# Decode step taken apart, full-depth Strassen in the heads and first convolutions, and two buffers resized by one slot and four tiles

## The chip, the cores and the metric

The kernel runs on one core of one Trainium2 chip. The metric is the device time of one execution in microseconds (us), lower is better. The kernel before was timed three times: 2169.92, 2166.01 and 2169.59 us, median 2169.59 us. One further execution was recorded by the hardware profiler; all durations of single instructions below are from that one.

## The reference, cut to what matters

Two layers of a decoder trunk run over 512 prompt positions and 8 sample streams of one new token each, with shared weights. All data is float32.

```python
h = rmsnorm(x, norm_g)
z = h @ w_in                       # 2048 x 8192: [B, C, xc, g_conv | q, k, v, g_ret]
conv = short_conv(c_c * x_c)       # width 3, causal
y_conv = b_c * conv * silu(g_c)
q, k = rope(q), rope(k) / 16       # 4 heads of 256
# one token per sample stream, S is the state (256 x 256) of a head:
inter = (q @ S) * gamma            # what the old state gives
intra = (q . k) * v                # what the new token gives itself
S_new = gamma * S + k^T v          # an output, for each layer, stream, head
y_ret = groupnorm(inter + intra) * gn_g * silu(g_r)
x = x + concat(y_conv, y_ret) @ w_out
x = x + sigmoid(x @ w_pg) * (p @ w_ple)
```

The prompt's retention goes in chunks; its arithmetic is not touched here. The sample streams have 2 layers x 4 heads x 8 streams = 64 states of 256 x 256 float32 (256 KB each); every one has to be read, updated and written out once.

## The kernel before, in words

**Layout.** Activations lie transposed: a tile ("slot") is 128 rows of the model dimension by 520 columns, 512 prompt positions and 8 samples. There are 75 slots, handed out first-in first-out (`Slots`, L80). The model dimension of 2048 is 16 tiles deep, here called 16 K tiles.

**A product in three.** Each float32 operand is split into a rounded high part and a remainder, by ScalarE (L229 for weights, L551 for activations) and VectorE (L230, L552). A product is then three TensorE matmuls, high x high, high x low and low x high (`mm3`, L247 to L249), each 128 x 128 by 260 columns, half a slot. Raw weights come in by DMA from the SyncE queue (L222, L312) into a ring of 32 tiles; the split weights go into a second ring of 60 tiles (`SPLIT`), each chunk of up to 4 tiles taking one range for the high and one for the low part.

**A pair of output tiles.** `pair` (L396) makes two output tiles of 128 rows by 520. With `rows[n]` = 0 it calls `plain` (L270): 16 K tiles x 2 outputs x 2 halves = 64 products. With `rows[n]` = s it calls `strassen` (L290): the first s K tiles go as 2 x 2 blocks with seven block products of s/2 products each, and the remaining 16 - s K tiles go plainly with four products each, so 7s/2 + 4(16 - s) products. Strassen needs sums of weight tiles, four passes over s/2 tiles on VectorE (L319), and sums of activation tiles, four tiles for each two K tiles, made once by `operand_sums` (L410) and kept in slots. For s < 16 it uses a fourth PSUM bank c, and two products' results are combined after the plain rest (L385 to L389); for s = 16 three banks do.

**Stages of a layer.** The lists HEADS, CONVS, OUT_ROWS and GATES (L53 to L59) hold s for each pair of each layer, in order.
- *Heads*: 4 heads x 4 pairs (q, k, v, gate), `head` (L801), `retain` (L817). The pairs that carry s = 14 are 12 in the first layer and 15 in the second.
- *Convolutions*: 8 x 2 pairs (L1077). The first two and the last have s = 14, the 13 between have s = 16.
- *OUT*: 8 pairs of the output projection (L1130).
- *GATE*: 8 pairs of the gated embedding in the first layer (L1175), 7 in the second, whose last two tiles go another way in the tail (from L1215).

Between pairs, and at fixed points inside them, short jobs are run from two lists: everything in `middle` near the middle of a pair (L365), and one job of `later` at two points of each pair (`aside`, L265). The prompt's retention is cut into nine steps per head that go through `later`. Activations of the next stage are made ahead by `fill` (L468) when slots are free, and by `need` (L483) when a pair can't do without them.

**The decode step before.** For each (head, stream): `sample_load` (L768) takes two slots and loads the state and, repeated on all 128 partitions, the rows for q and k from a DRAM tile kq. One call later `sample_step` (L774) scales the state by gamma on ScalarE (L776), adds k times v in two VectorE instructions (L780), sends the new state to o_rets (L781), and takes q times the new state, summed, in two more (L784, into `osum`). Everything of it lies in the heads and convolutions, from 50.5 us (the first state load) to 1731.3 us. In the last convolution `sample_norm` (L1364) normalises all of `osum`.

**What sets the order.** Instructions are not issued as written: a planner orders each engine's list by priority (order of writing, with weight splits and sums put ahead) and by the times at which it expects operands to be ready. Each engine then runs its list strictly in that order, and waits where an operand is late. All DMAs of activations and states go through the GpSimd queue (`SIDE`), in its own order.

## Time and profile before

| | |
|---|---|
| three runs, us | 2169.92, 2166.01, 2169.59 (median 2169.59) |
| profiled execution: span, first to last instruction, us | 2167.3 |
| TensorE matmuls | 17861, busy 2147.8 us (99%) |
| VectorE busy | 1896.1 us (87%) |
| ScalarE busy | 1264.5 us (58%) |
| GpSimd busy, with its DMA issues | 430.6 us (20%) |
| DMA | 387.31 MB, mean 179 GB/s |
| granted TensorE clock, mean | 0.999 |

The profile gives no other time of its own execution than the span; it lies between the lowest and the highest of the three runs. "Busy" is the union of an engine's instructions. A matmul of 260 columns is shown with some 0.28 us, but its successor starts 0.12 us after it: they are pipelined, so that the number of matmuls that start in a stretch says more than the busy share. A line of a group reads: source line, engine, operation, output <- inputs, shape and count, then busy time and mean duration of one, then the idle time of the engine ahead of these instructions and what ended it. A line of the windows gives, for a stretch, busy us and count of each engine, the granted clock, the DMA engines' busy share and their GB/s.

In this execution the first layer's heads run to about 400 us, its convolutions to about 715, OUT to about 890, GATE to about 1100; the second layer's to about 1460, 1790, 1960 and 2100, and the tail to the end.

### The profile page before, as it was taken

Reading aid. Unit: us, or ns where it says so; the run is one execution under the profiler, and the core shown is the slowest. Engines: PE = TensorE matmul, PEld = TensorE weight load, DVE = VectorE, ACT = ScalarE, POOL = GpSimd, SP = SyncE. Lnnn points to the kernel's source line nnn. Section 1 sums busy time; section 2 is a strip of 40 time slices with the busy share of each in tenths; the row PEclk is TensorE's granted clock in tenths of the full one; section 3 lists DMA queues with packets and bytes.
Section 4 is the critical chain, followed back from the end, with each engine's and each line's share of the span. In section 5 each row is a group of like instructions: output and inputs, shape, how many; then the busy total and the mean of one; then the engine's idle time right before and its main releaser. Section 6 shows DMA issues by size and latency. Waiting matters only on the chain. (4 is left out here: it accounts for less than half of the span.)

```text
span 2167.3 us, 48178 instructions
## 1 busy us (share of the span) xinstructions
PE 2147.8 (99%) x17861; PEld 2142.1 (99%) x17861; DVE 1896.1 (87%) x3849; ACT 1264.5 (58%) x2647; POOL 430.6 (20%) x746
## 2 busy tenths in 40 slices
PE   9999999999999999999999999999999999999998
PEld 9999999999999999999999999999999999999998
DVE  8889988998999987987997988989999998879884
ACT  8656655565555655655765655565645555456565
POOL 2313222211001211200212222231111022011011
PEclk9999999999999999999999999999999999999999
DMA  8555565545543745645645566664464355566455
GB/s 288 171 175 197 181 217 184 178 157 175 158 129 118 238 156 187 215 154 160 215 144 175 172 213 191 189 209 170 151 182 149 120 158 202 176 207 200 128 164 198
DMA packets 182861, 387.31 MB, mean 179 GB/s; under 512 B 25888, under 2 KB 56352, under 8 KB 182624
## 3 DMA queue, kind: packets, MB, share of 16 engines
q1 hardware_dynamic: 128704, 212.98, 31.6%
q0 software_dynamic: 53056, 169.84, 23.8%
q8 instruction: 140, 2.29, 0.4%
q10 hardware_dynamic: 864, 1.39, 0.2%
q14 instruction: 97, 0.79, 0.1%
HBM read 318.96 MB, written 65.15 MB: 177 GB/s over the span
## 5 line engine op out<-in xcount | busy, mean ns | idle before, releaser
L247 PE MATMUL ps_g<-slot,split 128*128 128x260 f32 x5465 | 1531.6, 284 | 7.2 <-ACT slot L307 2.9
L248 PE MATMUL ps_g<-slot,split 128*128 128x260 f32 x5465 | 1534.3, 282 | 0.3 <-DVE slot L555 0.3
L249 PE MATMUL ps_g<-slot,split 128*128 128x260 f32 x5461 | 1519.9, 283 | 0.5 <-DVE split L230 0.5
L229 ACT ACTIVATE split<-raw 128x512 fp32r<-128x512 f32 (+2 forms) x1347 | 777.3, 596 | 583.1 <-DVE raw L319 213.2
L247 PEld LDWEIGHTS ps_g<-slot,split 128*128 128x128 f32 x5465 | 1024.0, 188 | 10.1 <-ACT slot L307 3.7
L248 PEld LDWEIGHTS ps_g<-slot,split 128*128 128x128 f32 x5465 | 1028.5, 188 | 0.5 <-DVE slot L555 0.5
L249 PEld LDWEIGHTS ps_g<-slot,split 128*128 128x128 f32 x5461 | 1019.8, 188 | 1.0 <-DVE split L230 1.0
L230 DVE TENSOR_TENSOR split<-raw,split 128x512 fp32r<-128x512 f32 (+2 forms) x1346 | 849.2, 652 | 172.5 <-PE ps_g L248 85.4
L319 DVE TENSOR_TENSOR raw<-raw 128x512 f32<-128x512 f32 (+1 forms) x660 | 428.9, 660 | 32.5 <-DMA raw<-wi 23.7
L307 ACT ACTIVATE slot<-ps_g 128x260 f32<-128x260 f32 x336 | 127.4, 381 | 140.6 <-PE ps_g L249 122.7
L551 ACT ACTIVATE slot<-slot 128x520 fp32r<-128x520 f32 (+1 forms) x212 | 109.2, 562 | 46.6 <-DVE slot L414 11.1
L552 DVE TENSOR_TENSOR slot<-slot,slot 128x520 fp32r<-128x520 f32 (+1 forms) x212 | 124.4, 620 | 4.1 <-ACT slot L551 3.9
L781 POOL DMA_DIRECT2D o_rets<-slot x64 | 35.3, 552 | 351.6 <-DVE slot L780 131.7
L307 DVE TENSOR_TENSOR slot<-ps_g,slot 128x260 f32<-128x260 f32 x168 | 70.9, 424 | 6.0 <-PE ps_g L249 3.7
L869 POOL DMA_DIRECT2D slot<-hs x64 | 46.2, 724 | 118.7 <-DVE split L230 42.7
L814 POOL DMA_DIRECT2D hs<-slot x64 | 35.6, 556 | 139.3 <-DVE slot L755 61.3
L780 DVE SCALAR_TENSOR_TENSOR slot<-slot,vs,slot 128x256 f32<-128x256 f32 x128 | 56.1, 481 | 4.5 <-ACT slot L776 4.3
L746 DVE TENSOR_TENSOR slot<-slot,slot 128x520 f32<-128x520 f32 x80 | 55.8, 698 | 4.7 <-DMA o_rets<-slot 3.7
L770 POOL DMA_DIRECT2D slot<-sret x64 | 35.5, 554 | 114.6 <-ACT split L229 37.3
L1058 POOL DMA_DIRECT2D slot<-x1s x76 | 40.8, 538 | 87.6 <-PE ps_g L249 27.2
L1209 POOL DMA_DIRECT2D x2s<-slot x30 | 16.4, 545 | 201.6 <-DVE slot L1204 200.6
L771 POOL DMA_DIRECT2D slot<-kq x64 | 34.9, 547 | 106.0 <-DVE slot L876 22.2
(217 smaller groups left out, 1733.8 us busy)
## 6 DMA issues: line engine op xcount, KB each, us to landing
raw<-wi SPq DMA_DIRECT2D x377, 256.0 KB, 3.9
raw<-wo SPq DMA_DIRECT2D x128, 256.0 KB, 5.4
raw<-wg SPq DMA_DIRECT2D x122, 256.0 KB, 4.1
raw<-wi SPq DMA_DIRECT2D x136, 192.0 KB, 4.0
slot<-x1s POOLq DMA_DIRECT2D x76, 260.0 KB, 5.1
slot<-sret POOLq DMA_DIRECT2D x64, 256.0 KB, 4.0
hs<-slot POOLq DMA_DIRECT2D x64, 256.0 KB, 4.0
slot<-hs POOLq DMA_DIRECT2D x64, 256.0 KB, 5.2
```

Source lines behind the costliest of these rows:

```text
L229: S.activation(hi, raw, AF.Copy)
L230: V.tensor_tensor(lo, raw, F(hi), SUB)
L247: PE.matmul(out, wh, xh, start=start, stop=False, skip_group_check=more)
L248: PE.matmul(out, wh, xl, start=False, stop=False, skip_group_check=more)
L249: PE.matmul(out, wl, xh, start=False, stop=stop, skip_group_check=more)
L307: fn(*args)
L319: V.tensor_tensor(out[:, n], x[:, n], y[:, n], op)
L551: keep(S.activation(hi, src[:, n], AF.Copy))
L552: V.tensor_tensor(lo, src[:, n], F(hi), SUB)
L746: V.tensor_tensor(out[:, n], v, table[:, n], MUL)
L780: keep(V.scalar_tensor_tensor(st[:, c], k, vs[:, h, e, b : b + 1], st[:, c], MUL, ADD))
L869: SIDE.dma_start(t[:, :512].rearrange("p (m n) -> p m n", m=2), src)
```

## The change

- **Rows of Strassen.** In the heads s becomes 16 where it was 14 (12 + 15 pairs), and in the convolutions of each layer the first two pairs go from 14 to 16 (2 x 2 pairs); the last stays 14. These are 31 pairs.
- **The decode step is taken apart.** In the heads and convolutions only gamma times q times the *old* state is taken (`sample_step`, two reducing VectorE instructions with gamma as a constant). The new token's own part, (q . k) v, is made for all streams at once in `sample_norm`: q times k elementwise into a new small tile `qk` (one VectorE instruction per head), summed over partitions by two float32 matmuls with ones of 32 columns each, times `vs`, added to `osum`.
- **The new states are made in OUT and GATE**, by `update`, a pipeline of three: `key_load` takes a slot and loads the k row, repeated on all partitions, into its right half; at the next call `state_add` makes k times v in two ScalarE instructions and issues a DMA that *adds* the old state from DRAM onto the slot; at the next call `state_out` scales by gamma on ScalarE and sends the slot to o_rets. `vs` now carries v / 16 / gamma, so that gamma (S + k v / gamma) is the new state. `update` is called in the middle and at the end of each pair of OUT and GATE and, in four of the eight OUT pairs, once more through `later`: 20 calls in OUT, 16 in the first layer's GATE and 14 in the second's, for 32 states and two calls of pipeline.
- **Loads.** One slot of queries now serves two streams.
- **Sizes.** 76 slots for 75, 56 split tiles for 60; the constant tile `vec` loses its gamma columns.

```diff
-NSLOT = 75
+NSLOT = 76
...
+GAMMA = [1.0 - 2.0 ** (-5 - h) for h in range(H)]
-HEADS = [[0, 0, 0, 8] + [14] * 12, [0] + [14] * 15]
-CONVS = [[14] * 2 + [16] * 13 + [14]] * 2
+HEADS = [[0, 0, 0, 8] + [16] * 12, [0] + [16] * 15]
+CONVS = [[16] * 15 + [14]] * 2
...
-SPLIT = 60
+SPLIT = 56
...
         def sample_load(h, b):
-            st, kb = get(), get()
+            st = get()
             SIDE.dma_start(st[:, :512], sret[l, h, b])
-            SIDE.dma_start(kb[:, :512], kq[l, h, b].rearrange("c d -> (c d)").partition_broadcast(P))
-            return h, b, st, kb
-
-        def sample_step(h, b, st, kb):
-            keep(S.activation(st[:, :512], st[:, :512], AF.Identity, scale=gam(h)))
-            k = kb[:, 256:512]
+            if b % 2 == 0:
+                queries.append(get())
+                src = kq[l, h, b : b + 2, :2].rearrange("b c d -> b (c d)").partition_broadcast(P)
+                SIDE.dma_start(queries[-1][:, :512].rearrange("p (b c) -> p b c", b=2), src)
+            return h, b, st, queries[-1]
+
+        def sample_step(h, b, st, q):
             for e in range(2):
                 c = slice(256 * e, 256 * e + 256)
-                keep(V.scalar_tensor_tensor(st[:, c], k, vs[:, h, e, b : b + 1], st[:, c], MUL, ADD))
-            SIDE.dma_start(o_rets[l, h, b], st[:, :512])
-            for e in range(2):
-                c = slice(256 * e, 256 * e + 256)
-                V.tensor_tensor_reduce(k, st[:, c], kb[:, :256], 1.0, 0.0, MUL, ADD, osum[:, e, h, b : b + 1])
-            put(st, kb)
+                n = slice(256 * (b % 2), 256 * (b % 2) + 256)
+                keep(V.tensor_tensor_reduce(st[:, c], st[:, c], q[:, n], GAMMA[h], 0.0, MUL, ADD, osum[:, e, h, b : b + 1]))
+            put(st)
+            if b % 2:
+                put(q)
...
+        def key_load(h, b):
+            st = get()
+            SIDE.dma_start(st[:, 256:512], kq[l, h, b, 2:].rearrange("c d -> (c d)").partition_broadcast(P))
+            return h, b, st
+
+        def state_add(h, b, st):
+            for e in range(2):
+                c = slice(256 * e, 256 * e + 256)
+                keep(S.activation(st[:, c], st[:, 256:512], AF.Copy, scale=vs[:, h, e, b : b + 1]))
+            SIDE.dma_start(st[:, :512], sret[l, h, b], accum_op=ADD)
+            return h, b, st
+
+        def state_out(h, b, st):
+            keep(S.activation(st[:, :512], st[:, :512], AF.Copy, scale=GAMMA[h]))
+            SIDE.dma_start(o_rets[l, h, b], st[:, :512])
+            put(st)
+
+        keyed, added = [], []
+
+        def update():
+            if added:
+                state_out(*added.pop(0))
+            if keyed:
+                added.append(state_add(*keyed.pop(0)))
+            if states:
+                keyed.append(key_load(*states.pop(0)))
+
+        states = [(h, b) for h in range(H) for b in range(NS)]
...
+            V.scalar_tensor_tensor(qk[:, :, h], qks[:, :2, :NS], GAMMA[h], qks[:, 2:, :NS], MUL, MUL)
...
-                V.scalar_tensor_tensor(vs[:, h, e, :], t[:, SEQ:T], 1.0 / 16, rb[:, SEQ:T], MUL, MUL)
+                V.scalar_tensor_tensor(vs[:, h, e, :], t[:, SEQ:T], 1.0 / 16 / GAMMA[h], rb[:, SEQ:T], MUL, MUL)
...
             middle.append(lambda: O.fill(MORE_OUT, 0))
+            middle.append(update)
+            if m % 4:
+                later.append(update)
             zs = pair(O, wo[l], m, m // 2, Gt)
+            update()
...
             middle.append(lambda: Gt.fill(MORE_GATE, 0))
+            middle.append(update)
...
             Gt.fill(MORE_GATE, 0)
+            update()
             Gt.need(m // 2 + 1)
...
-def sample_norm(nc, small, pr, osum, onesd, half_neg, gs, gn):
+def sample_norm(nc, small, pr, osum, qk, vs, ones, onesd, half_neg, gs, gn):
...
+    ps = pr.tile([P, 512], F32, tag="r", name="ps_qk")
+    for d in range(2):
+        PE.matmul(ps[:, :n], ones, qk[:, d].rearrange("p h b -> p (h b)"), start=d == 0, stop=d == 1)
+    own = small.tile([P, 2, H, NS], F32, tag="sq", name="own", bufs=1)
+    for e in range(2):
+        V.tensor_tensor(own[:, e], vs[:, :, e], ps[:, :n].rearrange("p (h b) -> p h b", b=NS), MUL)
+        V.tensor_tensor(osum[:, e], osum[:, e], own[:, e], ADD)
```

More of the change, by code (lines that the diff above doesn't have):

```diff
@@ L558, in split @@
         return op
-    vec = const.tile([P, 160], F32, name="vec")
+    vec = const.tile([P, P], F32, name="vec")
     def norm_g(l, k):
@@ L578, in kd @@
         return vec[:, c : c + 1]
-    def gam(h):
-        return vec[:, 128 + h : 129 + h]
     ident = const.tile([P, P], F32, name="ident")
@@ L590, in trunk_kernel @@
     osum = const.tile([P, 2, H, NS], F32, name="osum")
+    qk = const.tile([P, 2, H, NS], F32, name="qk")
     gs = const.tile([P, 2 * H, NS], F32, name="gs")
@@ L679, in trunk_kernel @@
             DMA.dma_start(raw.rearrange("p (m n) -> p m n", n=P), wi[0, 0:4, :, :P].rearrange("m p n -> p m n"))
-            S.dma_start(vec, vecs)
+            S.dma_start(vec, vecs[:, :P])
             x = get()
@@ L1104, in trunk_kernel @@
                 O.ready = 7
-                sample_norm(nc, small, pr, osum, onesd, half_neg, gs, lambda k: gn_g(l, k))
+                sample_norm(nc, small, pr, osum, qk, vs, ones, onesd, half_neg, gs, lambda k: gn_g(l, k))
             zg, zb = pair(X, wi[l], mt + 2, mt // 2 + 1 - skipped, O)
@@ L1359, in trunk_kernel @@
             block_out(1)
+        assert not (todo or loaded or states or keyed or added)
         if l < DEPTH - 1:
             X.ready = KT // 2
-def sample_norm(nc, small, pr, osum, onesd, half_neg, gs, gn):
+def sample_norm(nc, small, pr, osum, qk, vs, ones, onesd, half_neg, gs, gn):
     V, G, PE = nc.vector, nc.gpsimd, nc.tensor
```

2 lines of the change are left out of this document (1 added, 1 removed).

## The prediction

> **What bounds the kernel now.** I read the page's head first, then the groups of instructions by shape, then busy time by stage, and the waits and the chain last.
>
> ```profile
> span 2167.3 us, 48178 instructions
> ...
> PE 2147.8 (99%) x17861; PEld 2142.1 (99%) x17861; DVE 1896.1 (87%) x3849; ACT 1264.5 (58%) x2647; POOL 430.6 (20%) x746
> ```
>
> TensorE is busy 99%, which alone says little, since its matmuls overlap. The stretches below say how many start (the x behind PE); their columns are PE, PEld, DVE, ACT and POOL busy, clock, DMA share, GB/s.
>
> ```profile
> 200.00:250.00 50.00, 50.00 (x420) 50.00 (x419) 47.05 (x101) 30.28 (x67) 10.12 (x17) 1.00 0.60 184
> 60.00:400.00 340.00, 340.00 (x2837) 339.45 (x2837) 306.31 (x673) 201.48 (x443) 94.42 (x163) 1.00 0.59 188
> 400.00:700.00 300.00, 299.06 (x2498) 298.88 (x2497) 273.85 (x550) 164.63 (x334) 42.34 (x63) 1.00 0.49 150
> 700.00:730.00 30.00, 26.68 (x218) 26.07 (x218) 30.00 (x65) 24.88 (x68) 10.58 (x20) 1.00 0.81 272
> 730.00:890.00 160.00, 160.00 (x1337) 159.98 (x1336) 133.95 (x242) 84.92 (x169) 28.52 (x54) 1.00 0.59 192
> 890.00:1100.00 210.00, 210.00 (x1756) 210.00 (x1755) 183.43 (x361) 134.23 (x257) 33.83 (x63) 1.00 0.56 178
> 1100.00:1460.00 360.00, 359.39 (x2999) 358.41 (x2998) 317.89 (x697) 210.53 (x470) 93.21 (x156) 1.00 0.59 182
> 1460.00:1730.00 270.00, 269.12 (x2241) 268.08 (x2241) 246.83 (x493) 147.66 (x304) 37.01 (x63) 1.00 0.50 158
> 1775.00:1800.00 25.00, 23.15 (x191) 22.72 (x191) 24.66 (x55) 18.24 (x51) 7.99 (x15) 1.00 0.87 305
> ```
>
> In an undisturbed stretch 420 matmuls start in 50 us: one in 0.1190 us, 8.4 in a us. At that pace the two stretches of heads (second and seventh row) lack 2856 - 2837 = 19 and 3024 - 2999 = 25 matmuls, 5.2 us; the convolutions (third and eighth) 22 and 27, 5.8 us; the two passages into OUT (fourth and last) 34 and 19, 6.3 us; the OUT and GATE rows only 7 and 8. So TensorE's work sets the end: a matmul taken away is worth 0.119 us, and VectorE or ScalarE work taken away is worth something only out of those few lost microseconds.
>
> ```profile
> L247 PE MATMUL ps_g<-slot,split 128*128 128x260 f32 x5437 | 1523.6, 284 | 7.2 <-ACT slot L307 2.9 <-ACT ps_g L307 1.6 <-ACT split L229 1.5
> L230 DVE TENSOR_TENSOR split<-raw,split 128x512 fp32r<-128x512 f32 x1031 | 695.0, 690 | 147.8 <-PE ps_g L248 81.2 <-ACT split L229 51.8 <-issue 6.1
> L319 DVE TENSOR_TENSOR raw<-raw 128x512 f32<-128x512 f32 x520 | 354.1, 688 | 17.6 <-DMA raw<-wi 12.1 <-DMA raw<-wo 2.9
> L230 DVE TENSOR_TENSOR split<-raw,split 128x384 fp32r<-128x384 f32 x249 | 137.1, 555 | 16.2 <-ACT split L229 9.9 <-PE ps_g L248 3.4 <-ACT slot L551 1.9
> L319 DVE TENSOR_TENSOR raw<-raw 128x384 f32<-128x384 f32 x140 | 77.4, 554 | 14.9 <-DMA raw<-wi 11.6 <-DMA raw<-wg 2.8
> L230 DVE TENSOR_TENSOR split<-raw,split 128x256 fp32r<-128x256 f32 x66 | 27.3, 423 | 8.5 <-ACT split L229 7.6 <-PE ps_g L248 0.8
> L780 DVE SCALAR_TENSOR_TENSOR slot<-slot,vs,slot 128x256 f32<-128x256 f32 x128 | 56.1, 481 | 4.5 <-ACT slot L776 4.3
> L784 DVE CUSTOM_DVE_ANT_0 slot<-slot,slot 128x256 f32<-128x256 f32 x128 | 53.9, 421 | 0.0
> L776 ACT ACTIVATE slot<-slot,vec 128x512 f32<-128x512 f32 x64 | 45.7, 714 | 0.0
> L874 ACT ACTIVATE slot<-slot 128x512 fp32r<-128x512 f32 x48 | 28.7, 624 | 10.1 <-DMA yc<-slot 4.6 <-DVE slot L904 2.4 <-DVE osum L784 2.1
> L917 ACT ACTIVATE slot<-ps_kt,vec 128x256 fp32r<-128x256 f32 x32 | 15.0, 468 | 9.2 <-DMA hs<-slot 3.2 <-DVE slot L918 2.5 <-PE ps_kt L913 2.2
> ```
>
> The first row bears the count that the change acts on. A pair has 7s/2 + 4(16 - s) products (64 for s = 0): 57 at s = 14, 56 at s = 16. Summed over the lists of rows, with the 30 fourth products of the embedding that also go to these banks, that is 5437, the row's count. The weight splits on VectorE wait 81.2 us for TensorE (second row): the ring of split weights is usually full, VectorE is ahead.
>
> **The change, part by part.**
>
> *Strassen rows.* 31 pairs lose one product each, three matmuls: 93 x 0.119 = **11.1 us less**. This is the firm term. The Trainium skill (TensorE: Matmul & The Clock Gate, Back-to-back issue gap) gives N/2.4 + 2.5 ns for a warm isolated gap, by our estimate 110.8 ns at 260 columns and 10.3 us for the 93; the trace has 119.0 ns, and I keep that.
>
> VectorE pays for it. A pair's four sums and seven splits go over 8 tiles (4 + 4) in place of 7 (3 + 4), less the two plain chunks of 256 columns: 4 x (688 - 554) + 7 x (690 - 555) - 2 x 423 = 635 ns a pair, 20 us over 31 pairs. It lies beside matmuls, in stages where VectorE is busy 88 to 91%; without cover it would be 0.6 us a pair. ScalarE saves one bank copy a pair. Three PSUM banks in place of four leave one more free at each pair's end; I count nothing for it.
>
> *Sums made earlier.* The eighth pair of K tiles needs its sums before the second Strassen pair of the heads, where they could be made later. Two loads, two scalings, four half-tile sums and two splits, once a layer: nothing if `fill` has made them by then, some 3 us a layer in the worst case, as much as all that these heads now lose. I take 0.
>
> *The decode step leaves the heads and convolutions.* 128 instructions of L780 (56.1 us of VectorE) and 64 of L776 (45.7 us of ScalarE) go; the 128 of L784 stay, with a constant and another place to write. Some 16 small instructions of under 0.25 us come in. With the 20 us above, VectorE is relieved by about 33 us over the two layers, 11 in a layer's convolutions (some 13 of its 32 steps fall there). That can give back what waits there for VectorE: between 0 and the 5.8 us. The chain through the worst stretch shows both kinds of wait,
>
> ```profile
> 1693.65 0.68 DVE split L230
> 1694.33 0.61 DVE raw L319
> 1695.01 3.75 DMA raw<-wi
> ...
> 1706.59 0.88 DVE slot L780 x2
> ...
> 1717.32 3.63 DMA raw<-wi
> ```
>
> VectorE's queue and late raw weights, and only the first is helped: I take a third, **1.9 us less**.
>
> *sample_norm* gains two matmuls of 32 columns a layer, just like the pair that is there:
>
> ```profile
> 1734.53 0.53 PE L1371 MATMUL ps_sm<-osum,onesd 128*128 128x32 f32 x4
> 1734.89 0.37 PE L247 MATMUL ps_g<-slot,split 128*128 128x260 f32 x1
> ```
>
> Two calls are four instructions, 0.36 us to the next matmul's start, and that one's successor comes 0.08 us later than usual: 0.45 us a layer, **0.9 us more**. The rest of the chain there ends some 25 us before its result is read in OUT.
>
> *The new states in OUT and GATE.* For each state: two ScalarE instructions of 256 columns (nearest row L917, 468 ns) and one of 512 (L874, 624 ns), 1.56 us, 50 us a layer. ScalarE is busy 84.92 of 160 us in OUT and 134.23 of 210 in the first GATE; with 20 and 16 calls it would be 72 to 76%, still beside matmuls. On the GpSimd queue come three issues a state where one and a half (64 + 32 for 64 states) stay behind, each near 0.55 us: 192 issues, 106 us over the stages of OUT and GATE, where it is busy under a fifth. The queue is in order: the adding DMA waits for `state_add`, the store for `state_out`, and behind them stand the loads of the stage's activations, for which the splits at L551 wait, and TensorE at the next pair. ScalarE is in order too: `state_add` waits for its key row and `state_out` for the sum to land, and behind them stand weight splits. What covers both is the ring: 56 tiles are seven chunks high and low, 7 x 12 matmuls x 0.119 = 10.0 us ahead. With 60 tiles and chunks of four it was seven as well, so I cost the smaller ring at nothing.
>
> ```profile
> slot<-sret POOLq DMA_DIRECT2D x64, 256.0 KB, 4.0
> raw<-wo SPq DMA_DIRECT2D x128, 256.0 KB, 5.4
> ...
> DMA to landing us min/median/max: 2.8/4.0/7.3
> ...
> DMA to landing us min/median/max: 2.6/4.0/10.5
> ```
>
> These are the state's plain load, the raw weights of OUT, and the extremes of the states' loads (L770) and of the weights' (L312). No row shows a DMA that adds. From below it costs what the plain load does, 4.0 us; from above I double it, since it also reads what it adds to, 8 us as an estimate. Near either end one call to the next (3 to 9 us apart) covers most of it, and I take nothing for the bulk. DMA traffic per state is 128 + 256 + 256 KB: 20 states in OUT's 160 us are 80 GB/s on top of 192. The Trainium skill (DMA: Bandwidth & Descriptors, Issuing engines are not separate DMA queues) says that transfers from all queues interleave on the same 16 engines, which speaks against this change: weights from SyncE are not shielded from GpSimd's states. The passage into OUT is where this bites first: DMA is busy 0.81 and 0.87 there, and the chain runs through it:
>
> ```profile
> 1781.89 7.02 DMA slot<-ys
> ```
>
> Two or three `update` calls fall into each passage. Bounds: 0 to doubling the 6.3 us lost; I take **1 us more** for both.
>
> One slot more and one query slot for two streams ease waiting for slots in the heads; three states in flight take three slots in OUT and GATE. Neither shows in a wait of TensorE now; 0.
>
> **Sum**: -11.1 + 0.9 - 1.9 + 1.0 = -11.1 us. Against the profiled span: 2167.3 to 2156.2. The span lies inside the runs' 2166.0 to 2169.9, whose median is 2.3 us above it; with the median, **2158.5 us**.
>
> **The rivals.**
>
> *More is given back.* All that the convolutions and heads lose, 5.8 + 5.2 us, was waiting for VectorE and for banks, and the relief frees it: 2169.6 - 10.2 - 11.0 = 2148. For: VectorE at 91% there. Against: the raw-weight waits on the chain, and that the heads' VectorE load falls only by some 4%.
>
> *The passages eat it.* States compete with ys, yc and weights into OUT, and the late eighth sums cost their 3 us a layer: 6 + 5 more, 2169.6 - 10.2 + 11 = 2170. No change.
>
> *Weights land late in OUT (slower).* VectorE has 160 - 133.95 = 26 us free in OUT's eight pairs, 3.3 us a pair, and uses it to refill the ring after waiting for the third raw block of a pair. If the landing of raw<-wo rises from 5.4 by more than 3.3 us, to 8.7, each further microsecond is lost once a pair, 16 times. At 9.3 us the gain is gone; at 9.9, under the 10.5 already seen once for weights, 1.2 x 16 = 19 us are lost: 2169.6 - 10.2 + 19 = 2178. For: the added 80 GB/s, and the rule of the skill cited above. Against: in the 305 GB/s of the passage few matmuls are lost for weights.
>
> *ScalarE stands at state_out (slower).* ScalarE has 75 us free in OUT, 9.4 a pair; 2.5 calls use 3.9, so each call may stand 2.2 us. Half a microsecond beyond that for each of 64 states is 32 us: 2191. It needs the sum to land over 2 us after the planner's time.
>
> **How the numbers follow.** Forecast 0.50 (its own range 2153 to 2164), more given back 0.16, passages 0.13, late weights 0.13, ScalarE 0.08. 0.2% is 4.3 us, about what a measurement here can tell from no change. Faster 0.66; same 0.13; slower 0.21. Range: half of the second case and most of the fifth left out, the fourth's price at its upper part: 2149 to 2176.
>
> **What would show it.** The 260-column row of L247 should read x5406; the 384-column rows of L319 and L230 x16 and x32; L780's and L776's old groups gone; a window in mid-heads still 420 in 50 us. OUT's and GATE's windows should keep 8.35 matmuls a us or more with DMA at 0.7 to 0.85 and ScalarE near 0.75. The step on states is wrong if TensorE there waits for splits that stand behind a state on ScalarE, or if raw<-wo lands above 8.7 us; the relief is wrong if the convolutions still lack some 50 matmuls. The whole is wrong if the runs do not fall below 2165.

## The result, and the profile after

The changed kernel takes 2242.99 us (median of 4 runs, 2240.44 to 2245.27), the kernel before, run beside it, 2169.66 us: a ratio of 1.0343, with a 95% interval of 1.0329 to 1.0358. It is 73 us slower. The prediction said 2158.5 us, range 2149 to 2176; it was wrong in sign.

The head of the page of the profile after:

```profile
span 2238.6 us, 47968 instructions
...
PE 2156.8 (96%) x17776; PEld 2144.6 (96%) x17776; DVE 1881.7 (84%) x3675; ACT 1299.8 (58%) x2682; POOL 516.2 (23%) x842
```

There are 85 fewer matmuls than before (17861): the 93 are gone and 8 small ones came in. At 8.4 a microsecond they should give back 10.1 us; instead the span grew by 71.3. Groups of instructions by shape confirm the counts forecast: x5406 for the first row below, and x32 and x16 for the 384-column splits (L231) and sums (L320). Most lines of the kernel before have moved by one here, L247 to L248 and so on.

```profile
L248 PE MATMUL ps_g<-slot,split 128*128 128x260 f32 x5406 | 1522.2, 285 | 64.8 <-ACT slot L1234 36.2 <-ACT split L230 10.5 <-DVE slot L308 7.0
L808 ACT ACTIVATE slot<-slot 128x512 f32<-128x512 f32 x64 | 40.2, 628 | 85.2 <-DMA slot<-sret 85.2
L804 POOL DMA_DIRECT2D slot<-sret x64 | 57.0, 891 | 33.6 <-ACT slot L803 23.1 <-ACT slot L308 4.4 <-ACT slot L1093 3.2
```

The first row's idle time is new (64.8 us, 7.2 before): TensorE waits 36.2 us for L1234, the sigmoid of a GATE pair. The last two rows are the new state's scaling, which stands 85.2 us for the adding DMA to land, and that DMA's issue, 891 ns long.

Busy time by stage (columns as in the prediction: PE, PEld, DVE, ACT, POOL, clock, DMA share, GB/s):

```profile
60.00:400.00 340.00, 337.03 (x2797) 335.13 (x2797) 302.75 (x616) 184.35 (x382) 80.64 (x134) 1.00 0.53 167
400.00:700.00 300.00, 300.00 (x2507) 300.00 (x2506) 268.24 (x525) 159.28 (x323) 35.90 (x49) 1.00 0.44 136
700.00:760.00 60.00, 54.30 (x417) 53.18 (x416) 52.41 (x108) 39.52 (x99) 20.63 (x36) 0.94 0.73 234
760.00:925.00 165.00, 159.90 (x1313) 158.87 (x1313) 127.98 (x233) 98.37 (x203) 57.64 (x96) 0.99 0.79 240
925.00:952.00 27.00, 8.55 (x64) 8.20 (x63) 15.32 (x30) 13.64 (x26) 5.97 (x9) 0.71 0.38 89
1460.00:1730.00 270.00, 270.00 (x2262) 270.00 (x2262) 243.30 (x474) 149.61 (x304) 34.45 (x54) 1.00 0.48 146
1800.00:1850.00 50.00, 44.47 (x356) 42.86 (x356) 47.45 (x98) 35.30 (x89) 16.84 (x30) 1.00 0.71 229
1850.00:2025.00 175.00, 171.17 (x1417) 169.93 (x1416) 135.16 (x240) 102.89 (x207) 60.83 (x102) 1.00 0.80 244
2025.00:2052.00 27.00, 7.92 (x39) 7.26 (x39) 16.06 (x32) 14.15 (x27) 5.64 (x9) 0.63 0.36 79
```

Each stretch, read against 8.4 matmuls a microsecond, gives the time lost in it. The first layer's heads (first row) lack 59, where they lacked 19 before: 4.8 us more, of which the run with the old sizes below says more. The first layer's convolutions (second row) lack 13 and the second's (sixth) 6: the relief there came. Both passages into OUT (third and seventh) lack 87 and 64, that is 10.4 and 7.6 us. The rest of OUT (fourth and eighth) lacks 73 and 53, 15.0 us. The two passages from OUT to GATE (fifth and ninth) lack 163 and 188, **41.8 us**. In the kernel before, the OUT and first GATE stages around them lacked 7 and 8.

The hole of the first layer, in order of time. First GpSimd's queue: start, length, line, operation, and in brackets the idle time before it with what ended it.

```profile
917.84 0.55 POOL L1087 DMA_DIRECT2D slot<-x1s  x1 [3.56 <-DVE slot L417]
920.66 0.55 POOL L809 DMA_DIRECT2D o_rets<-slot  x1 [2.27 <-ACT slot L808]
921.60 0.88 POOL L804 DMA_DIRECT2D slot<-sret  x1 [0.40 <-ACT slot L803]
926.77 0.56 POOL L809 DMA_DIRECT2D o_rets<-slot  x1 [4.28 <-ACT slot L808]
927.32 0.57 POOL L1087 DMA_DIRECT2D slot<-x1s  x1
...
933.40 0.56 POOL L809 DMA_DIRECT2D o_rets<-slot  x1 [4.63 <-ACT slot L808]
934.35 0.86 POOL L804 DMA_DIRECT2D slot<-sret  x1 [0.38 <-ACT slot L803]
936.25 0.56 POOL L1087 DMA_DIRECT2D slot<-x1s  x1 [1.04 <-DMA o_rets<-slot]
939.27 0.54 POOL L809 DMA_DIRECT2D o_rets<-slot  x1 [2.46 <-ACT slot L808]
...
942.56 0.56 POOL L1087 DMA_DIRECT2D slot<-x1s  x1 [1.09 <-issue]
```

Then ScalarE and TensorE in the same stretch:

```profile
925.84 0.63 ACT L808 ACTIVATE slot<-slot 128x512 f32<-128x512 f32 x1 [1.88 <-DMA slot<-sret]
932.48 0.63 ACT L808 ACTIVATE slot<-slot 128x512 f32<-128x512 f32 x1 [3.48 <-DMA slot<-sret]
938.35 0.63 ACT L808 ACTIVATE slot<-slot 128x512 f32<-128x512 f32 x1 [3.79 <-DMA slot<-sret]
...
947.04 0.64 ACT L552 ACTIVATE slot<-slot 128x520 fp32r<-128x520 f32 x1 [3.69 <-DVE slot L415]
...
950.43 0.58 PE L248 MATMUL ps_g<-slot,split 128*128 128x260 f32 x1 [18.45 <-ACT slot L1234]
```

This is the loss in one picture. Several updates stand in a row. GpSimd's store (L809) waits for ScalarE's scaling (L808), which waits for the adding DMA (L804), which GpSimd could issue only after the store before it. One round takes about 6 us, and between two rounds at most a single load of x1s (L1087) passes; the one at 936.25 waits besides, for 1.04 us, until a store has left its slot. These loads bring the operands of the first GATE pairs. Their sums (L415) and so their splits (L552) come late, the sigmoid that empties the banks (L1234) stands behind those splits in ScalarE's order, and TensorE, which needs the banks, stands for 18.45 us. The matmuls after it start 0.22 us apart for some 3 us before they are back at 0.12 us (the granted clock of the stretch is 0.71).

### The profile page after: what moved, and what is told of

Read it like the earlier page. It is cut to its first block, busy times and chain, and to the rows that moved or that the text cites. A ratio compares the mean times of both kernels' runs of the same rounds, so it can differ in the third digit from the quotient of the medians.

```text
span 2238.6 us, 47968 instructions
## 1 busy us (share of the span) xinstructions
PE 2156.8 (96%) x17776; PEld 2144.6 (96%) x17776; DVE 1881.7 (84%) x3675; ACT 1299.8 (58%) x2682; POOL 516.2 (23%) x842
## 5 line engine op out<-in xcount | busy, mean ns | idle before, releaser
L248 PE MATMUL ps_g<-slot,split 128*128 128x260 f32 x5434 | 1530.2, 285 | 64.8 <-ACT slot L1234 36.2
L230 ACT ACTIVATE split<-raw 128x512 fp32r<-128x512 f32 (+1 forms) x1285 | 783.5, 624 | 698.3 <-PE ps_g L249 378.5
L248 PEld LDWEIGHTS ps_g<-slot,split 128*128 128x128 f32 x5434 | 1022.6, 189 | 72.5 <-ACT slot L1234 36.9
L231 DVE TENSOR_TENSOR split<-raw,split 128x512 fp32r<-128x512 f32 (+1 forms) x1284 | 857.1, 687 | 226.9 <-ACT split L230 212.5
L320 DVE TENSOR_TENSOR raw<-raw 128x512 f32<-128x512 f32 (+1 forms) x660 | 445.4, 685 | 42.9 <-DMA raw<-wo 21.2
L308 ACT ACTIVATE slot<-ps_g 128x260 f32<-128x260 f32 x336 | 124.0, 372 | 18.1 <-PE ps_g L250 10.1
L552 ACT ACTIVATE slot<-slot 128x520 fp32r<-128x520 f32 (+1 forms) x212 | 109.2, 562 | 37.0 <-DVE slot L415 14.2
L769 POOL DMA_DIRECT2D slot<-sret x64 | 35.7, 558 | 249.5 <-DVE osum L781 108.7
L808 ACT ACTIVATE slot<-slot 128x512 f32<-128x512 f32 x64 | 40.2, 628 | 85.2 <-DMA slot<-sret 85.2
L809 POOL DMA_DIRECT2D o_rets<-slot x64 | 35.0, 547 | 233.1 <-ACT slot L808 217.1
L804 POOL DMA_DIRECT2D slot<-sret x64 | 57.0, 891 | 33.6 <-ACT slot L803 23.1
L803 ACT ACTIVATE slot<-slot,vs 128x256 f32<-128x256 f32 x128 | 63.6, 497 | 0.5
L1087 POOL DMA_DIRECT2D slot<-x1s x76 | 43.9, 588 | 45.1 <-DVE slot L553 8.0
```

What stands on the lines that cost most here:

```text
L230: S.activation(hi, raw, AF.Copy)
L231: V.tensor_tensor(lo, raw, F(hi), SUB)
L248: PE.matmul(out, wh, xh, start=start, stop=False, skip_group_check=more)
L308: fn(*args)
L320: V.tensor_tensor(out[:, n], x[:, n], y[:, n], op)
L552: keep(S.activation(hi, src[:, n], AF.Copy))
```

## The experiments

All times are medians, timed beside the kernel before, whose own medians were 2167.5 to 2169.7 us.

### Which part costs

*The rows alone*: the kernel before with only the two lists of rows changed.

```diff
-HEADS = [[0, 0, 0, 8] + [14] * 12, [0] + [14] * 15]
-CONVS = [[14] * 2 + [16] * 13 + [14]] * 2
+HEADS = [[0, 0, 0, 8] + [16] * 12, [0] + [16] * 15]
+CONVS = [[16] * 15 + [14]] * 2
```

> Kernel before with the new lists of Strassen rows alone (31 pairs from 14 to 16 K tiles; 75 slots, 60 split tiles, decode step as before). If the 93 matmuls are worth 0.119 us each and nothing else moves: 11 us under before, some 2158 to 2160 us. If the earlier sums or the longer sums on VectorE cost what the changed kernel's heads lost (26 matmuls more than before in the first layer's heads): 2162 to 2166.

Measured: 2185.57 us, ratio 1.0075 (1.0059 to 1.0091). By themselves the rows cost 16 us, more than either theory had. The two layers' heads:

```profile
60.00:400.00 340.00, 330.82 (x2728) 328.27 (x2729) 307.48 (x631) 191.78 (x394) 93.82 (x160) 0.99 0.57 184
1100.00:1460.00 360.00, 351.09 (x2898) 348.19 (x2896) 323.68 (x654) 204.61 (x416) 91.73 (x153) 1.00 0.56 178
```

They lack 128 and 126 matmuls where they lacked 19 and 25: 210 more, 25.0 us, against the 11.1 us of the 93 that are gone. The loss is in the heads.

*Everything but the rows*: the changed kernel with the old two lists.

> Changed kernel with the old lists of rows (14 K tiles again), all else as changed. If the loss comes from the new states in OUT and GATE and the rows are worth their matmuls, it is 11 us above the changed kernel: 2250 to 2258. If the rows are what hurts, it comes down towards 2170.

Measured: 2267.23 us, 1.0448 (1.0432 to 1.0463). Inside the changed kernel the rows are worth 24 us, more than the 11.1 of their matmuls; by themselves they lose. In the first layer's heads (60 to 400 us) this run lacks 84 matmuls, against 59 in the changed kernel and 19 in the kernel before: the rest of the change costs the heads time too, with the old rows still more. The parts do not add up, and the experiments from here on start from the changed kernel.

*No new states*: the changed kernel without `update`'s work.

```diff
-        states = [(h, b) for h in range(H) for b in range(NS)]
+        states = []
```

> Changed kernel that never makes the new states of the sample streams (no update does anything: no key rows, no adding DMA, no store, o_rets stays unwritten). If the whole loss is the states' work in OUT and GATE: 2150 to 2160. If the heads and convolutions (76 slots, 56 split tiles, fewer VectorE instructions, another order) share in it: 2170 or more.

Measured: 2167.99 us, 0.9999 (0.9988 to 1.0010). So `update` in OUT and GATE costs 2243.0 - 2168.0 = 75 us, all of the loss, and the rest of the change is worth nothing as it stands.

### One link of the update at a time

*A plain load for the adding one*

```diff
-            SIDE.dma_start(st[:, :512], sret[l, h, b], accum_op=ADD)
+            SIDE.dma_start(st[:, :512], sret[l, h, b])
```

> Changed kernel whose adding DMA is a plain load of the same bytes that overwrites the slot (the new state is then only gamma times the old one; every wait and slot stays). If the adding itself is dear (its landing 5.6 us in the median against 4.0 for the plain load, its issue 0.88 us against 0.55): it falls by 30 us or more, to 2210 or below. If it is the place and the waits of any DMA there, or slots: within 10 us of the changed kernel.

Measured: 2214.33 us, 1.0204 (1.0186 to 1.0223): 29 us of the 75 are due to the DMA's adding. Its issue falls from a mean of 891 to 544 ns, and its landing from a median of 5.6 to 4.4 us.

*No scaling at the end*

```diff
-            keep(S.activation(st[:, :512], st[:, :512], AF.Copy, scale=GAMMA[h]))
```

> Changed kernel without ScalarE's scaling in state_out: the store goes out straight when the adding DMA has landed (the state lacks a factor gamma), so ScalarE never waits for that landing; the GpSimd queue does. If ScalarE standing at state_out is the main loss (85 us of such waits in the profile): 2185 or below. If slots, traffic or the GpSimd queue are: 2225 or above.

Measured: 2228.21 us, 1.0276 (1.0261 to 1.0291). Without the instruction on which ScalarE stood 85 us, 15 us come back; the store on GpSimd now waits for the landing itself, 143.5 us. ScalarE's standing is not the main cost.

*The store from ScalarE's queue*

```diff
-            SIDE.dma_start(o_rets[l, h, b], st[:, :512])
+            S.dma_start(o_rets[l, h, b], st[:, :512])
```

> Changed kernel with one edit: the store of a new state is issued by ScalarE, right behind its own scaling, and no longer by GpSimd. GpSimd stood 217 us in all at these stores in the changed kernel, with the loads of the stage's activations behind them; ScalarE's wait for the landing stays. If GpSimd's queue standing still is the main loss: 2205 or below. If traffic or ScalarE's wait is: within 10 us of 2243.

Measured: 2259.16 us, 1.0412 (1.0391 to 1.0432): 16 us worse, so neither theory had it. The edit did not free GpSimd's queue: it now stands at the adding DMA (L804), 132.1 us behind the products k times v (L803), which stand behind the scaling on ScalarE; and TensorE waits for the sigmoid as in the changed kernel, 36.5 us in two holes. What the stores in ScalarE's own order cost was not separated. No run takes the waits off GpSimd altogether, or puts the loads of x1s on another queue.

*Moves only*: no ScalarE instruction in the update at all, a plain load, and the store.

```diff
-            for e in range(2):
-                c = slice(256 * e, 256 * e + 256)
-                keep(S.activation(st[:, c], st[:, 256:512], AF.Copy, scale=vs[:, h, e, b : b + 1]))
-            SIDE.dma_start(st[:, :512], sret[l, h, b], accum_op=ADD)
+            SIDE.dma_start(st[:, :512], sret[l, h, b])
...
-            keep(S.activation(st[:, :512], st[:, :512], AF.Copy, scale=GAMMA[h]))
```

> Changed kernel whose states are only moved: key row, a plain load of the old state, its store; no ScalarE instruction and no adding (o_rets receives the old state). Slots, bytes but for the adding's read, and the GpSimd queue stay. If traffic, queue and slots alone cost: near 2200 or above. If the waits on ScalarE are the cause: 2170 to 2180.

Measured: 2247.08 us, 1.0357 (1.0339 to 1.0374), 4 us above the changed kernel. The update's ScalarE instructions are not needed for the loss: GpSimd's queue now waits for the landings itself. Its waits:

```profile
POOL slot L801 <- DMA slot<-kq: 120.4, 41, 5.3
POOL o_rets L805 <- DMA slot<-sret: 113.5, 45, 7.7
```

That is 234 us, about the 217.1 + 23.1 which GpSimd spent behind ScalarE in the changed kernel (L809 behind L808, L804 behind L803).

*Two slots held*: the kernel without states, with two slots taken through OUT and GATE.

> The kernel that makes no states (2168 us), with two slots taken away from the start of OUT to the end of GATE, as many as the pipeline of states holds between two calls; no DMA and no instruction added. If the lack of slots is what starves the passages into GATE: 2190 or more. If not: 2168 to 2174.

Measured: 2172.35 us, 1.0017 (1.0008 to 1.0027), 4 us above the kernel without states. Two slots less are a small part.

### Where the calls stand, and how many

*Away from the passages*: no call in the first and last OUT pair and the first GATE pair, three in each of the others.

```diff
-            middle.append(update)
-            if m % 4:
+            if 2 <= m <= 12:
+                middle.append(update)
...
-            update()
+            if 2 <= m <= 12:
+                update()
...
-            middle.append(update)
+            if m >= 2:
+                middle.append(update)
+                later.append(update)
...
-            update()
+            if m >= 2:
+                update()
```

> Changed kernel with the calls of update moved: none in the first and last pair of OUT and none in the first of GATE, three in each other pair, so the same 64 states lie between the passages of stages. If the loss is made where states meet the passages' own loads (18 and 21 us of lost matmuls at the two passages into GATE): 2190 to 2205. If states cost wherever they are in OUT and GATE: within 10 us of 2243.

Measured: 2222.55 us, 1.0253 (1.0235 to 1.0271). The two long holes are gone (the stretch from 900 to 950 us has 409 matmuls, 11 short), but the same 64 states in fewer pairs lose time all along: between 750 and 900 us 110 matmuls are missing, from 950 to 1130 us 105, from 1830 to 2000 us 110 and from 2050 to 2150 us 98, 12 to 13 us in each OUT and each GATE. 20 us come back, 55 stay: between the marks of the two theories.

*In the convolutions*: two calls in each of the 16 pairs, one stage earlier, and the last of the pipeline after them.

```diff
@@ convolutions, in each pair
+            middle.append(update)
...
+            update()
...
@@ after the last of them
+        while states or keyed or added:
+            update()
...
@@ OUT and GATE, in each pair
-            middle.append(update)
-            if m % 4:
-                later.append(update)
...
-            update()
```

> Changed kernel with update called in the convolutions (middle and end of each of their 16 pairs) in place of OUT and GATE. DMA is busy 0.4 to 0.55 there, VectorE has been relieved, ScalarE has 45% free. If OUT and GATE are the wrong place because their loads are needed at once: 2170 to 2185. If the states' transfers and waits cost the same anywhere: 2230 or more.

Measured: 2217.42 us, 1.0222 (1.0198 to 1.0245): 49 us instead of 75, again between the marks. The convolutions do not take them for nothing either.

*Half of the states*: 32 of 64, with the calls at the pairs' ends left out.

```diff
-        states = [(h, b) for h in range(H) for b in range(NS)]
+        states = [(h, b) for h in range(H) for b in range(0, NS, 2)]
...
-            update()
...
-            update()
```

> Changed kernel with every second state left out (32 of 64 states are made; calls only in the middle of the pairs and through the later list, one pipeline as before). If the cost is in proportion to the states: half of the 75 us, 2200 to 2212. If it is a matter of overload in some stretches: 2180 or below.

Measured: 2182.44 us, 1.0065 (1.0048 to 1.0082). Half the states cost 14 us, not half of 75: the second half costs 61. Fewer updates stand in a row, and there are no long holes: 410 and 403 of 420 matmuls start at 880 to 930 and 1960 to 2010 us, in the passages to GATE.

### Bytes, or the chain of waits

*The same bytes without dependences*: key row, state and store as three DMAs on three held slots, nothing waiting for anything.

```diff
+                h, b = states.pop(0)
+                SIDE.dma_start(held[0][:, :256], kq[l, h, b, 2:].rearrange("c d -> (c d)").partition_broadcast(P))
+                SIDE.dma_start(held[1][:, :512], sret[l, h, b])
+                SIDE.dma_start(o_rets[l, h, b], held[2][:, :512])
```

> The kernel that makes no states, with three slots held from OUT to GATE and, at each call of update, the same three DMAs on the GpSimd queue (128 KB key row, 256 KB plain load, 256 KB store), but between slots that nothing else uses, so that none of them waits for another's landing or for ScalarE. The stored states are zeros. If bytes and issues cost: 2210 or more. If only the chain of waits (key row, load, store) does: 2172 to 2182, as with two slots held and no DMA (2172).

Measured: 2232.54 us, 1.0294 (1.0279 to 1.0309). This run does not decide. With nothing to wait for, the planner moved the 32 stores of a layer to the start of OUT; and the loads, all into the same two slots, waited for each other, 75.6 and 50.5 us of GpSimd's queue. So its bytes are not spread, and it is not free of a chain. One thing it does show, in two stretches:

```profile
740.00:790.00 50.00, 46.48 (x379) 45.44 (x378) 36.61 (x67) 21.55 (x43) 28.61 (x53) 1.00 0.94 325
890.00:940.00 50.00, 49.13 (x411) 48.93 (x410) 43.94 (x93) 29.61 (x59) 23.18 (x43) 1.00 0.95 322
```

At a DMA share of 0.94 to 0.95 TensorE lacks 41 matmuls of 420 in one and only 9 in the other. A full DMA stretch alone does not stop it.

*Fewer bytes*: the adding DMA and the store move 128 of 512 columns, 256 KB a state instead of 640; every instruction, wait and issue stays.

```diff
-            SIDE.dma_start(st[:, :512], sret[l, h, b], accum_op=ADD)
+            SIDE.dma_start(st[:, :128], sret[l, h, b, :, :128], accum_op=ADD)
...
-            SIDE.dma_start(o_rets[l, h, b], st[:, :512])
+            SIDE.dma_start(o_rets[l, h, b, :, :128], st[:, :128])
```

> Changed kernel in which the adding DMA and the store move only the first 128 of a state's 512 columns (64 KB each in place of 256); every call, instruction, slot and wait stays, and the rest of the state is left out. If bytes on the DMA engines are the cause: 2195 or below. If issues, waits and slots are: within 15 us of 2243.

Measured: 2200.87 us, 1.0151 (1.0135 to 1.0166). 64 x 384 KB = 25.2 MB fewer take 42 us away; 33 remain with 16.8 MB. That lies between the two marks: bytes count, and they are not all.

*Bytes alone*: the kernel before, with one plain load of 256 KB at each call's place, 16.8 MB.

```diff
+                st = get()
+                SIDE.dma_start(st[:, :512], sret[l, *states.pop(0)])
+                put(st)
```

> The kernel before, and at each call place of the new update in OUT and GATE one plain load of 256 KB of an old state into a slot that is taken and given back at once, 64 loads, 16.8 MB, read by nobody and waited for by no instruction but the slot's next use. Theory (bytes on the shared DMA engines in these stages make the loads that TensorE needs late; 24.6 MB fewer took 42 us away, 1.7 us a MB): 20 to 30 us more than before, 2188 to 2200. Rival (the chain of waits of the update through ScalarE and GpSimd is what costs, and bytes only by its landing times): within 5 us of before, 2165 to 2175.

Measured: 2172.72 us, 1.0022 (1.0012 to 1.0032): 4.8 us by the interval's middle. My theory of that moment (bytes) asked for 20 to 30 and fell.

*The chain with hardly any bytes*: the same as "fewer bytes", now with 64 columns for key row, state and store, 96 KB a state, 6.3 MB.

```diff
-            SIDE.dma_start(st[:, 256:512], kq[l, h, b, 2:].rearrange("c d -> (c d)").partition_broadcast(P))
+            SIDE.dma_start(st[:, :64], kq[l, h, b, 2, :64].partition_broadcast(P))
...
-            SIDE.dma_start(st[:, :512], sret[l, h, b], accum_op=ADD)
+            SIDE.dma_start(st[:, :64], sret[l, h, b, :, :64], accum_op=ADD)
...
-            SIDE.dma_start(o_rets[l, h, b], st[:, :512])
+            SIDE.dma_start(o_rets[l, h, b, :, :64], st[:, :64])
```

> The changed kernel with all 64 updates, their issues, ScalarE instructions, slots and waits in place, but key row, adding DMA and store move 64 of their 256 or 512 columns each: 96 KB a state in place of 640, 6.3 MB in all; so the key row and the new state are right only in part, and most of o_rets is not written. Points so far: without the states 2168.0 us, with 256 KB a state 2200.9, with 640 KB 2243.0. Theory (the loss goes with the bytes, 33 us over 16.8 MB): 6.3 MB x 2.0 us a MB = 13 us over the kernel without states, 2176 to 2186. Rival (a fixed cost of the chain of waits, whatever it moves, of some 28 us, since 16.8 MB without the chain cost 4.8 us): 2194 to 2202.

Measured: 2203.96 us, 1.0159 (1.0140 to 1.0177): 36 us above the kernel without states, a little over the upper end of what the fixed chain asked for, and no less than with 16.8 MB. So some 36 us come with the chain, whatever it moves; its waits, its issues and its ScalarE instructions are in it together. Its stages at the four passages,

```profile
700.00:760.00 60.00, 53.60 (x417) 51.71 (x416) 53.30 (x110) 40.25 (x101) 20.13 (x36) 0.97 0.67 208
920.00:945.00 25.00, 12.80 (x94) 12.60 (x94) 18.07 (x36) 14.80 (x29) 7.20 (x13) 0.73 0.25 56
1770.00:1845.00 75.00, 67.35 (x540) 66.10 (x539) 63.79 (x129) 46.35 (x113) 22.11 (x39) 0.98 0.65 198
2000.00:2025.00 25.00, 13.23 (x101) 13.02 (x100) 18.20 (x36) 13.85 (x26) 5.50 (x9) 0.80 0.16 33
```

and the same places in the kernel without states:

```profile
700.00:760.00 60.00, 56.73 (x451) 55.63 (x450) 55.47 (x117) 38.06 (x94) 16.29 (x30) 0.97 0.73 235
900.00:940.00 40.00, 40.00 (x337) 40.00 (x336) 33.27 (x64) 21.70 (x40) 3.83 (x7) 1.00 0.43 136
1740.00:1800.00 60.00, 56.75 (x451) 55.72 (x451) 54.75 (x118) 37.08 (x91) 12.66 (x22) 0.97 0.57 179
1960.00:2010.00 50.00, 50.00 (x420) 50.00 (x419) 41.95 (x82) 27.60 (x51) 6.33 (x12) 1.00 0.47 151
```

Above, 87, 116, 90 and 109 matmuls are missing, 47.9 us; below, 53, none, 53 and none, 12.6 us. The difference is 35.3 us, where these two profiled executions differ by 41.1 (2205.2 and 2164.1; the medians by 36.0): most of the fixed cost of the chain lies in the four passages, the larger part in the two to GATE. The rest of OUT adds to it, with 22 and 10 missing (760 to 920 and 1845 to 2000 us) against 3 and 5 without states (760 to 900 and 1800 to 1960). In the second and fourth row above the DMA share is 0.25 and 0.16, and more than half of the matmuls are missing: TensorE stands there with the DMA engines mostly idle. The wait there is for the order of two queues, not for bandwidth.

### The rows, the relief and the sizes

*The rows without the key's addition*: the rows alone, with the 128 VectorE instructions of L780 left out.

```diff
-            for e in range(2):
-                c = slice(256 * e, 256 * e + 256)
-                keep(V.scalar_tensor_tensor(st[:, c], k, vs[:, h, e, b : b + 1], st[:, c], MUL, ADD))
```

> The rows alone on the kernel before (2186 us), with the 128 VectorE instructions left out that add k times v to the states (the states and the sample streams' results are then wrong by it). That relieves VectorE by 56 us. If the rows fail because VectorE is full in the heads (0.1127 us of VectorE work per matmul there, against 0.1080 before and 0.119 for a matmul): 2155 to 2165. If slots, banks or earlier sums are the cause: 2178 or more.

Measured: 2164.60 us, 0.9979 (0.9969 to 0.9988). 56 us less of VectorE work are worth 21 us once the rows are there.

*That addition on other engines*: two ScalarE products into one more slot and one GpSimd addition.

```diff
+            kv = get()
             for e in range(2):
                 c = slice(256 * e, 256 * e + 256)
-                keep(V.scalar_tensor_tensor(st[:, c], k, vs[:, h, e, b : b + 1], st[:, c], MUL, ADD))
+                keep(S.activation(kv[:, c], k, AF.Copy, scale=vs[:, h, e, b : b + 1]))
+            keep(G.tensor_tensor(st[:, :512], st[:, :512], kv[:, :512], ADD))
+            put(kv)
```

> The kernel before with the new rows of heads and convolutions, its decode step in place, but with k times v made by two ScalarE instructions into an extra slot and added by one GpSimd instruction, in place of two VectorE instructions a state. Theory (VectorE's queue in the heads is what kept the rows alone from paying: leaving its 128 instructions out brought them from 2185.6 to 2164.6 us): 2162 to 2170 us. Rival (what counts is the work itself and its slots, on whichever engine): 2180 to 2195 us, the rows alone or worse.

Measured: 2193.10 us, 1.0101 (1.0076 to 1.0126), no better than leaving it on VectorE (1.0059 to 1.0091); the intervals overlap, so that it is worse is not shown. The group of VectorE's splits, first in the rows alone, then here:

```profile
L230 DVE TENSOR_TENSOR split<-raw,split 128x512 fp32r<-128x512 f32 x1248 | 834.4, 686 | 178.9 <-PE ps_g L248 92.2 <-ACT split L229 68.2 <-issue 11.6
```

```profile
L230 DVE TENSOR_TENSOR split<-raw,split 128x512 fp32r<-128x512 f32 x1248 | 870.8, 712 | 159.3 <-PE ps_g L248 104.9 <-ACT split L229 36.3 <-issue 9.8
```

The splits take 26 ns more on average, 36 us of VectorE for the 56 that were moved away. One such place, with GpSimd's addition at L782:

```profile
472.94 2.12 DVE L230 TENSOR_TENSOR split<-raw,split 128x512 fp32r<-128x512 f32 x1
473.20 1.30 POOL L782 TENSOR_TENSOR slot<-slot,slot 128x512 f32<-128x512 f32 x1
```

Of the 1248 splits, 65 overlap one of GpSimd's 64 additions; they take 1202 ns in the mean. The other 1183 take 685 ns, like all of them in the rows alone (686). The Trainium skill (Perfetto Trace Analysis, Optimizing Scalar/DVE Operations) says that GpSimd and VectorE share an SBUF read port, so that moving work between them may not help; these overlaps agree. So the longer splits come with GpSimd's additions, and not with the extra slot or ScalarE's two products. Whether the whole time is due to them was not separated.

*The old sizes*: the kernel without states, with 75 slots and 60 split tiles.

```diff
-NSLOT = 76
+NSLOT = 75
...
-SPLIT = 56
+SPLIT = 60
```

> The kernel that makes no states (2168 us), with the old sizes again, 75 slots and 60 split tiles. If the smaller ring of split weights takes away what the rows bring there: 2158 to 2163. If sizes do not matter, within 3 us of 2168; if the slot matters more than the ring, above it.

Measured: 2162.99 us, 0.9975 (0.9965 to 0.9985), 5.0 us below the kernel without states. The two layers' heads, with 60 tiles and then with 56:

```profile
60.00:400.00 340.00, 338.92 (x2831) 338.24 (x2830) 306.96 (x622) 189.23 (x387) 80.38 (x136) 1.00 0.52 167
1100.00:1460.00 360.00, 359.90 (x3003) 359.17 (x3002) 324.68 (x649) 201.56 (x412) 79.64 (x128) 1.00 0.52 166
```

```profile
60.00:400.00 340.00, 337.11 (x2802) 335.53 (x2802) 303.45 (x617) 184.93 (x382) 80.31 (x133) 1.00 0.52 167
1100.00:1460.00 360.00, 359.24 (x2991) 357.92 (x2990) 323.07 (x643) 198.41 (x410) 80.43 (x129) 1.00 0.52 166
```

29 + 12 = 41 matmuls more with the old sizes, 4.9 us: as much as the medians differ by. The two profiled executions differ by only 2.3 us (2161.8 and 2164.1), as other stretches shift: from 700 to 760 us the old sizes have 26 matmuls fewer, 425 to 451. So the gain in the heads is seen, but not that it is all of the 5.0 us; and the ring was not separated from the 76th slot.

### The balance

| step | us | from |
|---|---|---|
| before | 2169.7 | |
| rows, decode relief, own part in `sample_norm`, at the old sizes | -6.7 | 2163.0, without states |
| 76 slots and 56 tiles | +5.0 | 2168.0, without states |
| the update's chain of waits, 6.3 MB | +36.0 | 2204.0 |
| its other 35.6 MB | +39.0 | 2243.0 |

The last two overlap: 10.5 MB more on top of the 6.3 cost nothing (2200.9), and the 25.2 beyond that 42 us. A slower landing that lengthens each round of the chain fits this: the adding DMA lands after 4.0 and 3.7 us in the median with 32 and 64 KB and after 5.6 with 256 KB, and in the first passage to GATE the stores follow each other after 4.4 to 6.1 us in the few-bytes kernel and after 5.9 to 6.6 in the changed one. That this is the whole of the 42 us is argued, not shown. The changed kernel has 59.8 us missing in the four passages (10.4, 19.4, 7.6 and 22.4), the few-bytes kernel 47.9, the kernel without states 12.6; the 15.0 us of the rest of OUT come in beside.

No version tried beats the kernel before with all of its work done.

## Why the prediction was wrong

**The step that failed** is the one on the new states in OUT and GATE: "Near either end one call to the next (3 to 9 us apart) covers most of it, and I take nothing for the bulk", with 1 us for the two passages into OUT. Measured: 75 us, for all of the update. Three things in it were wrong.

*The cover.* I named the ring of split weights, 10.0 us ahead, as what covers a stall on GpSimd or ScalarE. It covers weights. What stands behind the store on GpSimd are the loads of activations, and the first pairs of a stage need all of theirs at once. The text even had the path ("behind them stand the loads of the stage's activations") and did not cost it.

*The place.* I priced only the passage into OUT. Of the passage from OUT to GATE nothing was said, since before it loses nothing; it became the largest loss, 41.8 us. Several updates meet there, and the loads of x1s have to pass between them.

*The length of a round.* I bounded the landing by 4 and 8 us; it came out as 3.6 at least, 5.6 in the median and 9.4 at most. But a round is not a landing. It is store, issue of 0.9 us (forecast near 0.55), landing, scaling and the next store, 6 us on two queues which wait for each other, so calls 3 us apart cannot all be kept. The waits of the changed kernel show it (engine and line, what ended the wait, us in all, times, longest):

```profile
POOL o_rets L809 <- ACT slot L808: 217.1, 50, 11.5
ACT slot L808 <- DMA slot<-sret: 85.2, 39, 7.6
PE ps_g L248 <- ACT slot L1234: 36.2, 3, 18.4
```

The total of the first row does not set the loss: in the few-bytes kernel GpSimd stands nearly as long at these stores, 202.4 us. What counts is where it stands, with the loads of GATE's operands behind it. That is traced in the holes, 41.8 us; the rest of the 75 us is for the most part located, in OUT, but not traced link by link.

**Strassen rows, -11.1.** The count was right, and so were VectorE's prices (691 ns for a split of 512 columns, 688 for a sum). That these 20 us were hidden was wrong where the relief is missing: the rows alone cost 16 us, lost in the heads. "Without cover it would be 0.6 us a pair", 20 us in all, was nearer: -11.1 + 20 gives 9 us more, measured 16.

**The relief, -1.9.** More came than forecast: in the kernel without states at old sizes the two heads lack 25 and 21 matmuls, about as before, with full rows; the convolutions of the changed kernel lack 19 where they lacked 49, 3.6 us. That is the rival "more is given back" in part, and its condition was met. It was still eaten: that kernel stands at 2163.0, not at 2148, and the one large loss seen in it is at the passages into OUT. They lack 79 and 58 matmuls there (700 to 760 and 1740 to 1820 us), 36 and 22 before: 9.4 us more. In the first the chain runs through a load of ys of 5.89 us, VectorE's splits and sums of OUT's operands, and a load of yc of 4.68 us. That is the place of the rival "the passages eat it", but with no new state made; why the loss grew there stays open.

**The smaller ring, 0, and the slot, 0.** Together wrong by 5.0 us. "Seven as well" counted whole chunks only; whether the four tiles beyond them are what was missed was not run.

**sample_norm, +0.9, and sums made earlier, 0.** Neither was measured alone; both are inside the -6.7.

**The rivals.** Late weights had its threshold at 8.7 us; the landings stayed below, though they rose (5.4 and 4.1 before):

```profile
raw<-wo SPq DMA_DIRECT2D x128, 256.0 KB, 6.4
raw<-wg SPq DMA_DIRECT2D x122, 256.0 KB, 5.9
```

So with states on GpSimd's queue SyncE's weights land later, as the rule of the Trainium skill cited in the prediction (DMA: Bandwidth & Descriptors, Issuing engines are not separate DMA queues) has it; but 16.8 MB of bare loads cost only 4.8 us. ScalarE at state_out was nearest: ScalarE does stand there, 85.2 us, 2.2 us in each of 39 waits but 1.3 over all 64 states, under the 2.2 that it had to spare. Without that instruction 15 us come back, half of the 32 that it asked for; the mechanism seen in the largest holes, GpSimd's store ahead of the loads of the next stage's activations, was no rival of mine.

**What would have shown it beforehand.** Counting, at each passage, the calls and the loads that share GpSimd's queue. In the hole shown above four stores of new states and four loads of x1s stand in 25 us of it, and each store carries a wait.

## What to carry to other kernels

A wait put into an in-order queue costs what stands behind it, so list that queue's own work stage by stage, above all at the passage where the next stage's first operands are fetched: it is there that a hidden chain turns into an idle TensorE. A chain of dependent steps across two in-order queues has a round time, and calls closer together than a round pile up; here half as many states cost a fifth. Whether bytes or order cost is told apart by two small runs, the bytes without the chain and the chain without the bytes.

## What the runs showed of the hardware that was not expected

- A DMA that adds onto its target took 884 ns (median) to issue from GpSimd against 545 ns for a plain load, with 32 KB (878 ns) as with 256 KB, and 64 of them in place of plain loads cost 29 us here.
- A DMA share of 0.95 at 322 GB/s for 50 us left TensorE at 411 of 420 matmuls; in 25 us at a share of 0.16 to 0.25, with a blocked queue, fewer than half of them started.
- After 18 us of idling TensorE's matmuls started 0.22 us apart for some 3 us instead of 0.12, so that this hole cost more than its length.
- An elementwise addition of 128x512 on GpSimd took 1.71 us in the mean, and the 65 of VectorE's splits that overlapped one took 1.20 us in place of 0.685.
